# A two-layer decoder trunk: order of sums and passes in the second MLP matrix, zero-padded differential scores

## The chip, the cores and the metric

The kernel runs on one core of a Trainium2 chip. It is written with a tile framework whose scheduler decides the order of the instructions on each engine. The metric is the device time of one execution in microseconds; the kernel before takes 2158.03 us (median of 3 runs, 2157.67 to 2158.33).

## The reference

The input x is 256 positions by 2048 channels, in float32. Two layers each do the following (S = 256, D = 2048, hidden width 8192):

```python
h = rms_norm(x, attn_norm_g[l])
proj = h @ w_in[l]                      # 2048 -> 3*768 + 3*768 + 2*512
moba_o = moba_attention(...)            # 6 heads x 128, causal here, since one block of 256 holds all positions
diff_o = diff_attention(...)            # 6 heads, q and k in two halves of 64:
                                        # softmax(q1 k1 / 8) - lambda * softmax(q2 k2 / 8), then norm
sgu_o = spatial_gating(...)             # 4 groups x 128 channels, causal mixing in chunks of 128 positions
x = x + concat(moba_o, diff_o, sgu_o) @ w_out[l]
h = rms_norm(x, mlp_norm_g[l])
x = x + square(relu(h @ w_mlp_in[l])) @ w_mlp_out[l]
```

A last RMSNorm follows. All results are float32.

## The kernel before

**Products.** Every float32 operand of a large product is split into a high part, rounded to the matrix engine's own 32-bit form, and a low part, the rest. A product is then three matmul passes of 512 columns: high by high, low by high, high by low. `halves` (L115) makes the two parts of a piece of weights: ACT copies the high part (L122, tiles `hi_...`), DVE subtracts it from the raw weights (L123, tiles `lo_...`), for two k-tiles of 128 rows at a time (128x1024). The tiles come from pools of four buffers each (`whl`), so ACT and DVE can prepare only a few pieces ahead of the matmuls.

**The MLP in chunks.** The hidden width is worked off in four chunks c of 2048 per layer. A chunk takes two blocks (g = 0, 1) of the first matrix (tiles named `..._h`) and then two blocks of the second (tiles named `..._o`), each of 1024 columns, by `gemm7` (L173). Over two layers this makes 16 blocks of each matrix.

**The block.** A block has two row halves t (128 positions each) and two column halves of 512, so four accumulators, each a PSUM bank: `pz` (t 0, first columns), `py` (t 0, second columns), `px` (t 1, first) and `pw` (t 1, second). Eight of the sixteen k-tiles are taken in four pairs by a scheme with seven products in place of eight. Its weights b11, b12, b21, b22 are four raw tiles of 128x2048 in three buffers (`rb_...`), and four sums of them are made on DVE in place (L200): t1 = b11+b12, t2 = t1+b22, t3 = b12+b22, t4 = t2+b21. In the first matrix t3 is made by a DMA that accumulates (`moved=True`). The products go to px and py in turn; `keep` takes an intermediate result out of its bank before the bank is used again (`ks1`, `kv2`, `ks5` and `kv3`; on ACT for the first three, L699, and for v3 on DVE into ks5, L695). The other eight k-tiles are "plain" products: `plain(half, i)` takes two of them against one column half, and writes the two banks of that half, three passes for each bank and k-tile (L215 to L217). I write plain(1, 0) as k-tiles (1,0), and lo_o(1,0) is the low part that goes with it. The first pass of px in plain(0, 0) overwrites px, so it must wait until v3 has been taken from it.

The order of writing in `gemm7` is: product b11 into px; t1 into py; plain (1,0), (1,1); t2 into px; plain (1,2); b22 into py; plain (1,3); t3 into px; plain (0,0), (0,1); t4 into px; plain (0,2); b21 into pz; plain (0,3). After the block, the caller adds each bank to its result: in the second matrix to the residual stream `xt`, times a per-row factor (L705), then adds the kept parts to it (by a DMA of POOL's queue that accumulates, or on DVE in the last chunk, L711).

**Work between the passes.** `pending` holds generators; `pump()` advances one of them, between products. In an o g0 block the last hidden tiles of the first matrix are transposed on PE (L257), copied to their high parts on ACT (L96) and subtracted on DVE (L97): tiles `hid011a`, `hid011b` in layer 0, chunk 1.

**What sets the order.** Each instruction is given a priority by the place in which it is written, and the scheduler, with its own estimate of when operands come ready, puts on each engine the ready one that was written first. `tc.issue_after(x)` keeps what is written under it from being put into the queue before instruction x. Each engine then runs its queue strictly in order.

**Scores.** For each head, `turned_qk` (L472) transposes q and k on PE and copies both with one ACT instruction (L480). `scores` (L465) takes q times k in two passes (L468, L469). For the differential heads it does so twice, with 64 of the 128 rows (partitions) each.

Of the kernel before, what the change touches and what calls it, by code (L numbers as in the profile page):

```python
# [41 lines left out]
def trunk(ctx: ExitStack, tc: tile.TileContext, x_in, xT, w_in, w_out, w_mlp_in, w_mlp_out,  # L42
# [130 lines left out]
    def gemm7(w, c0, lhs, sums, rest, keep, name, moved=False):  # L173
# [31 lines left out]
        def plain(half, i):  # L205
# [4 lines left out]
            for k, (hi, lo) in zip(ks, halves(raw[half][:, i % 2 * 2:i % 2 * 2 + 2, :], 2, f"{name}{half}{i}")):  # L210
                a, h = lhs[k]
                for t, ps in enumerate(((pz, px), (py, pw))[half]):
                    ah, al = a[:, h, t * P:(t + 1) * P], a[:, h, S + t * P:S + (t + 1) * P]
                    first, last = k == rest[0] and t == half, k == ks[-1]
                    T.matmul(ps, lhsT=ah, rhs=hi, start=first, stop=False, skip_group_check=True)  # L215
                    T.matmul(ps, lhsT=al, rhs=hi, start=False, stop=False, skip_group_check=True)  # L216
                    T.matmul(ps, lhsT=ah, rhs=lo, start=False, stop=last, skip_group_check=True)  # L217
                pump()

        b11, b12 = rawb(0, 0), rawb(0, 1)  # L220
# [11 lines left out]
        product(px, summed(0), halves(b11, SP, f"t2{name}"))  # L232
        keep("v2", px)
        plain(1, 2)
        product(py, summed(1), halves(b22, SP, f"b22{name}"))
        if not moved:
            add(b12, b22)
        plain(1, 3)
# [7 lines left out]
        plain(0, 2)  # L246
        product(pz, direct(1, 0), halves(b21, SP, f"b21{name}"))
        plain(0, 3)
        return [[pz, py], [px, pw]]
# [90 lines left out]
    for l in range(DEPTH):  # L340
# [27 lines left out]
        tabs = att.tile([P, 2, 4, 64], F32, tag="tabs", name=f"tabs_{l}", bufs=1)  # L368
# [80 lines left out]
        vh, qt, kt = {}, {}, {}  # L449

# [21 lines left out]
        def turned_qk(sec, h, name):  # L472
# [319 lines left out]
```

## Time and profile before

| | us |
|---|---|
| median of 3 runs | 2158.03 |
| lowest, highest | 2157.67, 2158.33 |
| the profiled execution | 2156.94 |
| its span in the trace | 2155.2 |
| PE busy (9500 matmuls) | 2115.4 (98%) |
| DVE busy (2036 instructions) | 1717.3 (80%) |
| ACT busy (1891 instructions) | 1354.7 (63%) |
| POOL busy (78 instructions) | 65.3 (3%) |
| mean granted clock of PE | 0.997 |

PE is TensorE, DVE VectorE, ACT ScalarE and POOL GpSimd. A row of a timeline has the start from the span's begin, the duration, the engine, the line of the code, the result and its operands with their shape, and in brackets the idle time of the engine ahead of it with the instruction that ended it. Matmuls overlap: a pass of 512 columns is listed with 0.39 us, but the next one starts 0.23 us later, so it is differences of starts that count.

### The profile page before, as it was taken

Reading aid. Unit: us, or ns where it says so; the run is one execution under the profiler, and the core shown is the slowest. Engines: PE = TensorE matmul, PEld = TensorE weight load, DVE = VectorE, ACT = ScalarE, POOL = GpSimd, SP = SyncE. Lnnn points to the kernel's source line nnn. Section 1 sums busy time; section 2 is a strip of 40 time slices with the busy share of each in tenths; the row PEclk is TensorE's granted clock in tenths of the full one; section 3 lists DMA queues with packets and bytes.
Section 4 is the critical chain, followed back from the end, with each engine's and each line's share of the span. In section 5 each row is a group of like instructions: output and inputs, shape, how many; then the busy total and the mean of one; then the engine's idle time right before and its main releaser. Section 6 shows DMA issues by size and latency. Waiting matters only on the chain. (4 is left out here: it accounts for less than half of the span.)

```text
span 2155.2 us, 25746 instructions
## 1 busy us (share of the span) xinstructions
PE 2115.4 (98%) x9500; PEld 1707.6 (79%) x9500; DVE 1717.3 (80%) x2036; ACT 1354.7 (63%) x1891; POOL 65.3 (3%) x78
## 2 busy tenths in 40 slices
PE   9999999999999999999999999999999999999997
PEld 7877888877877887787788778888778778878875
DVE  6665566898898888889965655668988988988897
ACT  6565564675676576676654655556756756766764
POOL 0000000000000000000000000000000000000000
PEclk9999999999999999999999999999999999999998
DMA  8644565657866866775465455656677568668652
GB/s 320 197 154 147 174 220 182 196 177 229 259 186 190 266 208 200 217 227 195 153 212 187 137 166 166 224 167 197 209 229 235 176 215 256 203 190 251 213 195 98
DMA packets 210893, 432.20 MB, mean 201 GB/s; under 512 B 7632, under 2 KB 8272, under 8 KB 208592
## 3 DMA queue, kind: packets, MB, share of 16 engines
q1 hardware_dynamic: 202416, 402.22, 56.5%
q0 software_dynamic: 7488, 26.22, 6.2%
q10 hardware_dynamic: 864, 2.14, 0.3%
q8 instruction: 74, 1.21, 0.2%
q14 instruction: 51, 0.42, 0.1%
HBM read 402.23 MB, written 2.10 MB: 188 GB/s over the span
## 5 line engine op out<-in xcount | busy, mean ns | idle before, releaser
L123 DVE TENSOR_TENSOR lo_wi<-raw_wi,hi_wi 128x1024 fp32r<-128x1024 f32 x160 | 195.0, 1222 | 161.9 <-ACT hi_wi L122 158.8
L122 ACT ACTIVATE hi_wi<-raw_wi 128x1024 fp32r<-128x1024 f32 x160 | 168.8, 1058 | 166.6 <-PE pg_wi L157 158.1
L156 PE MATMUL pg_wi<-hi_wi,xa 128*128 128x512 f32 x640 | 260.6, 407 | 0.0
L158 PE MATMUL pg_wi<-lo_wi,xa 128*128 128x512 f32 x640 | 251.7, 393 | 0.0
L157 PE MATMUL pg_wi<-hi_wi,xa 128*128 128x512 f32 x640 | 251.4, 393 | 0.0
L122 ACT ACTIVATE hi_o<-raw_o 128x1024 fp32r<-128x1024 f32 x128 | 135.6, 1059 | 62.9 <-PE pw_o L216 36.7
L122 ACT ACTIVATE hi_h<-raw_h 128x1024 fp32r<-128x1024 f32 x128 | 135.3, 1057 | 43.1 <-PE px_h L216 20.6
L123 DVE TENSOR_TENSOR lo_o<-raw_o,hi_o 128x1024 fp32r<-128x1024 f32 x128 | 155.4, 1219 | 6.6 <-ACT hi_o L122 5.3
L123 DVE TENSOR_TENSOR lo_h<-raw_h,hi_h 128x1024 fp32r<-128x1024 f32 x128 | 155.0, 1216 | 3.7 <-ACT hi_h L122 3.7
L200 DVE TENSOR_TENSOR rb_o<-rb_o,rb_o 128x2048 f32<-128x2048 f32 x64 | 146.4, 2287 | 10.5 <-DMA rb_o<-w_mlp_out 10.0
L156 PEld LDWEIGHTS pg_wi<-hi_wi,xa 128*128 128x128 f32 x640 | 120.4, 188 | 29.0 <-issue 7.3
L158 PEld LDWEIGHTS pg_wi<-lo_wi,xa 128*128 128x128 f32 x640 | 120.4, 188 | 25.0
L157 PEld LDWEIGHTS pg_wi<-hi_wi,xa 128*128 128x128 f32 x640 | 120.6, 188 | 22.4 <-issue 0.7
L123 DVE TENSOR_TENSOR lo_wo<-raw_wo,hi_wo 128x1024 fp32r<-128x1024 f32 x64 | 78.4, 1225 | 60.8 <-ACT hi_wo L122 60.8
L200 DVE TENSOR_TENSOR rb_h<-rb_h,rb_h 128x2048 f32<-128x2048 f32 x48 | 109.7, 2286 | 0.6
L122 ACT ACTIVATE hi_wo<-raw_wo 128x1024 fp32r<-128x1024 f32 x64 | 67.9, 1060 | 64.0 <-PE pg_wo L157 58.0
L156 PE MATMUL pg_wo<-hi_wo,mix 128*128 128x512 f32 x192 | 76.3, 398 | 0.0
L158 PE MATMUL pg_wo<-lo_wo,mix 128*128 128x512 f32 x192 | 75.1, 391 | 0.0
L157 PE MATMUL pg_wo<-hi_wo,mix 128*128 128x512 f32 x192 | 74.8, 390 | 0.0
L123 DVE TENSOR_TENSOR lo_b11h<-rb_h,hi_b11h 128x1024 fp32r<-128x1024 f32 x32 | 39.2, 1225 | 27.8 <-ACT hi_b11h L122 25.8
L122 ACT ACTIVATE hi_b11h<-rb_h 128x1024 fp32r<-128x1024 f32 x32 | 34.0, 1063 | 33.9 <-PE px_h L216 13.3
L123 DVE TENSOR_TENSOR lo_t1h<-rb_h,hi_t1h 128x1024 fp32r<-128x1024 f32 x32 | 38.6, 1221 | 19.6 <-ACT hi_t1h L122 19.6
(1937 smaller groups left out, 5855.3 us busy)
## 6 DMA issues: line engine op xcount, KB each, us to landing
raw_wi<-w_in SPq DMA_DIRECT2D x80, 1024.0 KB, 5.2
rb_h<-w_mlp_in SPq DMA_DIRECT2D x64, 1024.0 KB, 5.8
raw_h<-w_mlp_in SPq DMA_DIRECT2D x64, 1024.0 KB, 7.0
raw_o<-w_mlp_out SPq DMA_DIRECT2D x64, 1024.0 KB, 6.6
rb_o<-w_mlp_out SPq DMA_DIRECT2D x64, 1024.0 KB, 6.4
raw_wo<-w_out SPq DMA_DIRECT2D x24, 1024.0 KB, 5.2
rb_h<-rb_h POOLq DMA_DIRECT2D x16, 1024.0 KB, 6.9
raw_wo<-w_out SPq DMA_DIRECT2D x16, 512.0 KB, 5.0
```

What stands on the lines that cost most here:

```text
L122: A.activation(hi, raw[:, i:i + m, :], AF.Copy)
L123: V.tensor_tensor(lo, raw[:, i:i + m, :], hi.bitcast(F32), op=ALU.subtract)
L156: T.matmul(ps[t], lhsT=ah, rhs=hi, start=first, stop=False)
L157: T.matmul(ps[t], lhsT=al, rhs=hi, start=False, stop=False)
L158: T.matmul(ps[t], lhsT=ah, rhs=lo, start=False, stop=last)
L200: V.tensor_tensor(dst, dst, src, op=ALU.add)
```

## The change

Four things change.

1. In `gemm7` of the second matrix (`moved` not set), the sum t3 = b12+b22 is no longer written after the product b22 but after `halves` of t2, under `issue_after`, so that it is queued behind the last low part of t2. `halves` notes that instruction in `last_lo`.
2. `plain` writes its passes in pieces of one k-tile and one bank. For i = 0 it takes both k-tiles for the bank that is free, and only then both for the other (`order`); for i > 0 k-tile by k-tile as before.
3. `gemm7` calls `second(py, pw)` when the second 512 columns are complete, after plain(0, 0) is written; the caller's `update(1, ...)` then adds py and pw to xt there, ahead of the sum t4 and not after the block. For the first matrix `second` only hands the banks back.
4. For the differential heads q goes into two tiles of 128 rows each, of which the other half's 64 rows are zero (`halfq`, set by four memsets per layer on POOL), by two ACT copies of 64x256, and k into a tile of its own, by one ACT copy of 128x256. `scores` then takes all 128 rows.

Besides, the scaled rotary table is written over the unscaled one.

```diff
@@ halves
-            V.tensor_tensor(lo, raw[:, i:i + m, :], hi.bitcast(F32), op=ALU.subtract)
+            made = V.tensor_tensor(lo, raw[:, i:i + m, :], hi.bitcast(F32), op=ALU.subtract)
...
+        last_lo[0] = made.ins
@@ gemm7, plain
-            for k, (hi, lo) in zip(ks, halves(...)):
-                a, h = lhs[k]
-                for t, ps in enumerate(((pz, px), (py, pw))[half]):
-                    (three passes)
-                pump()
+            parts = list(zip(ks, halves(...)))
+
+            def piece(k, hi, lo, t):
+                a, h = lhs[k]
+                ps = ((pz, px), (py, pw))[half][t]
+                (three passes)
+
+            order = [(0, 0), (0, 1), (1, 0), (1, 1)] if i else [(j, t) for t in (half, 1 - half) for j in (0, 1)]
+            for n, (j, t) in enumerate(order):
+                k, (hi, lo) = parts[j]
+                piece(k, hi, lo, t)
+                if n % 2:
+                    pump()
@@ gemm7, body
         plain(1, 0)
         plain(1, 1)
-        product(px, summed(0), halves(b11, SP, f"t2{name}"))
+        t2 = halves(b11, SP, f"t2{name}")
+        if not moved:
+            with tc.issue_after(last_lo[0]):
+                add(b12, b22)
+        product(px, summed(0), t2)
         keep("v2", px)
...
         product(py, summed(1), halves(b22, SP, f"b22{name}"))
-        if not moved:
-            add(b12, b22)
...
         plain(0, 0)
+        second(py, pw)
         add(b11, b21)
@@ differential scores
+        halfq = []
+        for i in range(2):
+            z = att.tile([P, 2, S], F32, tag=f"halfq{i}", name=f"halfq{l}{i}", bufs=1)
+            G.memset(z[64:, 0], 0.0)
+            G.memset(z[:64, 1], 0.0)
+            halfq.append(z)
...
+            if sec == "d":
+                z = halfq[h % len(halfq)]
+                k = stage["att"].tile([P, S], F32, tag="dk", name=f"dk_{name}", bufs=2)
+                for i, rows in enumerate((slice(0, 64), slice(64, P))):
+                    A.activation(z[rows, i], pT[rows, :S], AF.Copy)
+                A.activation(k, pT[:, S:], AF.Copy)
+                return z[:, 0], z[:, 1], k
@@ second matrix, caller
-                ps = gemm7(w2[...], ..., f"o{l}{c}{g}")
-                for half in (1, 0):
+                def update(half, ps, c=c, g=g, kept=kept, xg=xg):
...
+                update(0, gemm7(w2[...], ..., lambda *ps, update=update: update(1, ps), f"o{l}{c}{g}"))
```

What this does to the queues, in an o g0 block (layer 0, chunk 1). On DVE, from the last sum that the first matrix leaves to the low part of the second plain pair, the order before is this (`rb_o_5212` is b11 and the sums made in it, `rb_o_5214` is b12, `rb_o_5248` is b22):

```order
L678 TENSOR_TENSOR ks1h_4862<-ks1h_4862,pz_h_4826 128x512
L200 TENSOR_TENSOR rb_o_5214<-rb_o_5214,rb_o_5248 128x2048
L123 TENSOR_TENSOR lo_t1o_0_5251<-rb_o_5212,hi_t1o_0_5250 128x1024
L123 TENSOR_TENSOR lo_t1o_2_5255<-rb_o_5212,hi_t1o_2_5254 128x1024
L97 TENSOR_TENSOR hid011b_5269<-pT_hid011b_5264,hid011b_5269 128x2x256
L97 TENSOR_TENSOR hid011a_5283<-pT_hid011a_5278,hid011a_5283 128x2x256
L200 TENSOR_TENSOR rb_o_5212<-rb_o_5212,rb_o_5248 128x2048
L123 TENSOR_TENSOR lo_o_0_5292<-raw_o_5289,hi_o_0_5291 128x1024
L97 TENSOR_TENSOR hid011b_5306<-pT_hid011b_5301,hid011b_5306 128x2x256
L97 TENSOR_TENSOR hid011a_5320<-pT_hid011a_5315,hid011a_5320 128x2x256
L123 TENSOR_TENSOR lo_o_0_5324<-raw_o_5289,hi_o_0_5323 128x1024
```

And this is the order of the change there (b11 is `rb_o_5229`, b12 `rb_o_5231`, b22 `rb_o_5265`):

```order
L125 TENSOR_TENSOR lo_t1o_0_5268<-rb_o_5229,hi_t1o_0_5267 128x1024
L125 TENSOR_TENSOR lo_t1o_2_5272<-rb_o_5229,hi_t1o_2_5271 128x1024
L204 TENSOR_TENSOR rb_o_5229<-rb_o_5229,rb_o_5265 128x2048
L97 TENSOR_TENSOR hid011b_5286<-pT_hid011b_5281,hid011b_5286 128x2x256
L97 TENSOR_TENSOR hid011a_5300<-pT_hid011a_5295,hid011a_5300 128x2x256
L125 TENSOR_TENSOR lo_o_0_5309<-raw_o_5306,hi_o_0_5308 128x1024
L97 TENSOR_TENSOR hid011b_5323<-pT_hid011b_5318,hid011b_5323 128x2x256
L97 TENSOR_TENSOR hid011a_5337<-pT_hid011a_5332,hid011a_5337 128x2x256
L125 TENSOR_TENSOR lo_o_0_5341<-raw_o_5306,hi_o_0_5340 128x1024
L125 TENSOR_TENSOR lo_t2o_0_5357<-rb_o_5229,hi_t2o_0_5356 128x1024
L125 TENSOR_TENSOR lo_t2o_2_5361<-rb_o_5229,hi_t2o_2_5360 128x1024
L204 TENSOR_TENSOR rb_o_5231<-rb_o_5231,rb_o_5265 128x2048
```

The sum of b12 and b22 has gone from the place ahead of lo_t1 to the one behind the last lo_t2, and the sum for t2 has gone ahead of the two hid conversions.

On DVE further on in the same block, about the sum for t4 (with b21, `rb_o_5436`), the order before:

```order
L123 TENSOR_TENSOR lo_t3o_0_5417<-rb_o_5214,hi_t3o_0_5416 128x1024
L123 TENSOR_TENSOR lo_t3o_2_5421<-rb_o_5214,hi_t3o_2_5420 128x1024
L200 TENSOR_TENSOR rb_o_5212<-rb_o_5212,rb_o_5436 128x2048
L123 TENSOR_TENSOR lo_o_0_5444<-raw_o_5441,hi_o_0_5443 128x1024
L123 TENSOR_TENSOR lo_o_0_5461<-raw_o_5441,hi_o_0_5460 128x1024
L123 TENSOR_TENSOR lo_t4o_0_5477<-rb_o_5212,hi_t4o_0_5476 128x1024
L695 TENSOR_TENSOR ks5o_5287<-ks5o_5287,px_o_5208 128x512
L123 TENSOR_TENSOR lo_t4o_2_5481<-rb_o_5212,hi_t4o_2_5480 128x1024
```

And that of the change (b21 is `rb_o_5453`):

```order
L125 TENSOR_TENSOR lo_t3o_0_5434<-rb_o_5231,hi_t3o_0_5433 128x1024
L125 TENSOR_TENSOR lo_t3o_2_5438<-rb_o_5231,hi_t3o_2_5437 128x1024
L125 TENSOR_TENSOR lo_o_0_5461<-raw_o_5458,hi_o_0_5460 128x1024
L738 SCALAR_TENSOR_TENSOR xt_79<-py_o_5226,r_0_3494,xt_79 128x512
L738 SCALAR_TENSOR_TENSOR xt_80<-pw_o_5228,r_0_3494,xt_80 128x512
L204 TENSOR_TENSOR rb_o_5229<-rb_o_5229,rb_o_5453 128x2048
L729 TENSOR_TENSOR ks5o_5304<-ks5o_5304,px_o_5225 128x512
L125 TENSOR_TENSOR lo_o_0_5482<-raw_o_5458,hi_o_0_5481 128x1024
```

The updates of xt from py and pw now stand ahead of that sum, and ks5, which frees px, directly behind it.

On PE at the first plain passes of the same block, before:

```order
L169 MATMUL py_o_5209<-lo_t1o_2_5255,hid010b_4943 128x512
L215 MATMUL pw_o_5211<-hi_o_0_5291,hid011b_5269 128x512
L216 MATMUL pw_o_5211<-hi_o_0_5291,hid011b_5269 128x512
L215 MATMUL py_o_5209<-hi_o_0_5291,hid011b_5269 128x512
L216 MATMUL py_o_5209<-hi_o_0_5291,hid011b_5269 128x512
L167 MATMUL px_o_5208<-hi_t2o_0_5339,e_hid010a_4919 128x512
L217 MATMUL py_o_5209<-lo_o_0_5292,hid011b_5269 128x512
L217 MATMUL pw_o_5211<-lo_o_0_5292,hid011b_5269 128x512
```

And in the change the end of plain(1, 1) and the start of t2:

```order
L223 MATMUL py_o_5226<-lo_o_0_5341,hid011b_5323 128x512
L221 MATMUL pw_o_5228<-hi_o_0_5340,hid011b_5323 128x512
L222 MATMUL pw_o_5228<-hi_o_0_5340,hid011b_5323 128x512
L223 MATMUL pw_o_5228<-lo_o_0_5341,hid011b_5323 128x512
L170 MATMUL px_o_5225<-hi_t2o_0_5356,e_hid010a_4936 128x512
L171 MATMUL px_o_5225<-hi_t2o_0_5356,e_hid010a_4936 128x512
L172 MATMUL px_o_5225<-lo_t2o_0_5357,e_hid010a_4936 128x512
L170 MATMUL px_o_5225<-hi_t2o_0_5356,e_hid010a_4994 128x512
```

The first pass of t2 stood behind the first two passes of py; it now stands behind all passes of plain(1, 0) and plain(1, 1).

## Rows read from the trace of the kernel before

**Rows 1.** page part 1: busy us, share of the span, instructions.

```profile
PE 2115.4 (98%) x9500; PEld 1707.6 (79%) x9500; DVE 1717.3 (80%) x2036; ACT 1354.7 (63%) x1891; POOL 65.3 (3%) x78
```

**Rows 2.** windows: stretch, length, busy us (x count) per engine, PEclk, DMA.

```profile
593.50:637.40 43.90, 43.77 (x198) 35.18 (x198) 41.47 (x54) 33.65 (x45) 0.86 (x1) 1.00 0.67 200
637.40:683.50 46.10, 43.95 (x197) 35.24 (x196) 40.13 (x35) 29.43 (x34) 1.75 (x2) 1.00 0.64 205
```

**Rows 3.** waits of PE: line, releaser, total us, times, longest.

```profile
PE px_o L167 <- ACT hi_t2o L122: 10.1, 9, 1.3
PE px_o L215 <- DVE ks5o L695: 5.9, 15, 0.6
PE py_o L215 <- ACT ks5o L699: 3.0, 9, 1.2
```

**Rows 4.** timeline of PE, o g0: start us, duration, instruction, idle before.

```profile
645.30 0.39 PE L216 MATMUL pw_o<-hi_o,hid011b 128*128 128x512 f32 x1
645.93 0.50 PE L215 MATMUL py_o<-hi_o,hid011b 128*128 128x512 f32 x1 [0.23 <-ACT ks5o L699]
646.26 0.40 PE L216 MATMUL py_o<-hi_o,hid011b 128*128 128x512 f32 x1
647.88 0.50 PE L167 MATMUL px_o<-hi_t2o,e_hid010a 128*128 128x512 f32 x1 [1.22 <-ACT hi_t2o L122]
...
668.01 0.39 PE L216 MATMUL pz_o<-hi_o,hid011b 128*128 128x512 f32 x1
668.86 0.50 PE L215 MATMUL px_o<-hi_o,hid011b 128*128 128x512 f32 x1 [0.46 <-DVE ks5o L695]
```

**Rows 5.** timeline of ACT, the same block.

```profile
638.75 1.04 ACT L122 ACTIVATE hi_t1o<-rb_o 128x1024 fp32r<-128x1024 f32 x1
...
646.77 2.01 ACT L122 ACTIVATE hi_t2o<-rb_o 128x1024 fp32r<-128x1024 f32 x2
```

**Rows 6.** timeline of DVE, the same block.

```profile
638.79 2.28 DVE L200 TENSOR_TENSOR rb_o<-rb_o,rb_o 128x2048 f32<-128x2048 f32 x1
640.99 2.35 DVE L123 TENSOR_TENSOR lo_t1o<-rb_o,hi_t1o 128x1024 fp32r<-128x1024 f32 x2
...
644.46 2.28 DVE L200 TENSOR_TENSOR rb_o<-rb_o,rb_o 128x2048 f32<-128x2048 f32 x1
646.66 1.21 DVE L123 TENSOR_TENSOR lo_o<-raw_o,hi_o 128x1024 fp32r<-128x1024 f32 x1
...
652.40 1.21 DVE L123 TENSOR_TENSOR lo_o<-raw_o,hi_o 128x1024 fp32r<-128x1024 f32 x1
...
662.51 2.29 DVE L200 TENSOR_TENSOR rb_o<-rb_o,rb_o 128x2048 f32<-128x2048 f32 x1 [0.73 <-DMA rb_o<-w_mlp_out]
...
668.12 0.68 DVE L695 TENSOR_TENSOR ks5o<-ks5o,px_o 128x512 f32<-128x512 f32 x1
```

**Rows 7.** timeline of PE, o g1 of the same chunk.

```profile
709.76 0.39 PE L215 MATMUL pz_o<-hi_o,hid011b 128*128 128x512 f32 x1
710.38 0.50 PE L215 MATMUL px_o<-hi_o,hid011b 128*128 128x512 f32 x1 [0.23 <-DVE ks5o L695]
```

**Rows 8.** timeline of PE, last o g1 of layer 0.

```profile
1038.72 0.50 PE L215 MATMUL py_o<-hi_o,hid031b 128*128 128x512 f32 x1 [1.16 <-ACT ks5o L699]
```

**Rows 9.** timeline of PE around a score pair of 64 rows.

```profile
129.21 0.40 PE L158 MATMUL pg_wi<-lo_wi,xa 128*128 128x512 f32 x1
...
130.72 0.39 PE L157 MATMUL pg_wi<-hi_wi,xa 128*128 128x512 f32 x1
```

**Rows 10.** timeline of PE around a score pair of 128 rows.

```profile
237.12 0.40 PE L158 MATMUL pg_wi<-lo_wi,xa 128*128 128x512 f32 x1
...
238.23 0.39 PE L157 MATMUL pg_wi<-hi_wi,xa 128*128 128x512 f32 x1
```

**Rows 11.** groups of ACT by form: busy us, mean ns, idle before.

```profile
L480 ACT ACTIVATE qk_d<-pqk_d 128x512 f32<-128x512 f32 x12 | 6.9, 590 | 6.4 <-PE pqk_d L478 6.4
...
L96 ACT ACTIVATE mix<-po_m 128x256 fp32r<-128x256 f32 x12 | 4.5, 376 | 3.7 <-PE po_m L541 3.7
```

More of the change, by code (lines that the diff above doesn't have):

```diff
@@ L113, in load @@
         return raw
+    last_lo = [None]
     def halves(raw, n, name):
@@ L171, in product, with gemm7 @@
                 pump()
-    def gemm7(w, c0, lhs, sums, rest, keep, name, moved=False):
+    def gemm7(w, c0, lhs, sums, rest, keep, second, name, moved=False):
         def rawb(two, half):
@@ L209, in plain @@
             ks = rest[2 * i:2 * i + 2]
-            for k, (hi, lo) in zip(ks, halves(raw[half][:, i % 2 * 2:i % 2 * 2 + 2, :], 2, f"{name}{half}{i}")):
+            parts = list(zip(ks, halves(raw[half][:, i % 2 * 2:i % 2 * 2 + 2, :], 2, f"{name}{half}{i}")))
+            def piece(k, hi, lo, t):
                 a, h = lhs[k]
-                for t, ps in enumerate(((pz, px), (py, pw))[half]):
[L213 to L217, printed above, removed]
-                pump()
+                ps = ((pz, px), (py, pw))[half][t]
+                ah, al = a[:, h, t * P:(t + 1) * P], a[:, h, S + t * P:S + (t + 1) * P]
+                first, last = k == rest[0] and t == half, k == ks[-1]
+                T.matmul(ps, lhsT=ah, rhs=hi, start=first, stop=False, skip_group_check=True)
+                T.matmul(ps, lhsT=al, rhs=hi, start=False, stop=False, skip_group_check=True)
+                T.matmul(ps, lhsT=ah, rhs=lo, start=False, stop=last, skip_group_check=True)
+            order = [(0, 0), (0, 1), (1, 0), (1, 1)] if i else [(j, t) for t in (half, 1 - half) for j in (0, 1)]
[4 more added lines that the diff above has]
+                    pump()
+        n = len(rest) // 2
         b11, b12 = rawb(0, 0), rawb(0, 1)
@@ L231, in gemm7 @@
         plain(1, 1)
-        product(px, summed(0), halves(b11, SP, f"t2{name}"))
+        t2 = halves(b11, SP, f"t2{name}")
[3 more added lines that the diff above has]
+        product(px, summed(0), t2)
         keep("v2", px)
-        plain(1, 2)
+        for i in range(2, n - 1):
+            plain(1, i)
         product(py, summed(1), halves(b22, SP, f"b22{name}"))
-        if not moved:
-            add(b12, b22)
-        plain(1, 3)
+        plain(1, n - 1)
         product(px, summed(2), halves(b12, SP, f"t3{name}"))
@@ L245, in gemm7 @@
         product(px, direct(1, 1), halves(b11, SP, f"t4{name}"))
-        plain(0, 2)
+        for i in range(2, n - 1):
+            plain(0, i)
         product(pz, direct(1, 0), halves(b21, SP, f"b21{name}"))
-        plain(0, 3)
-        return [[pz, py], [px, pw]]
+        plain(0, n - 1)
+        return pz, px
     def turned(src, c, name, tag="m"):
@@ L265, in turn @@
             d = pair(f"{name}{i}")
-            if sums is not None and (k0 + i) // 2 < SP:
+            if sums is not None and (k0 + i) // 2 < len(sums):
                 a = stage["mlp"].tile([P, 2, S], F32, tag="a", name=f"a_{name}{i}", bufs=1)
@@ L365, in trunk @@
         rc = rstd(ss_a, f"a{l}")
-        tabs = att.tile([P, 2, 4, 64], F32, tag="tabs", name=f"tabs_{l}", bufs=1)
+        tabs = ropet
         for t in range(2):
@@ L463, in softmax, with scores @@
             return e, sm
-        def scores(qk, rows, name):
+        def scores(q, k, name):
             pS = bank(f"ps_{name}", "s")
-            q, k = qk[rows, :S], qk[rows, S:]
             T.matmul(pS[:, 0:P], lhsT=q[:, 0:P], rhs=k[:, 0:P], start=True, stop=True)
@@ L716, in trunk @@
                         pending.append(turn(xa, xt, q * GW, 4 * q, f"xa{l + 1}_{q}_", C_ATT + (l + 1) * KT))
+                update(0, gemm7(w2[c * fw:(c + 1) * fw], 2 * g * GW, Want(hid), Want(hs), late, keep,
+                                lambda *ps, update=update: update(1, ps), f"o{l}{c}{g}"))
         close_mlp.close()
```

29 lines of the change are left out of this document (15 added, 14 removed).

## Prediction

> **What bounds the kernel now.** I read the first part of the page first: TensorE (PE) is busy 2115.4 us of the span of 2155.2 [rows 1]. So there are 39.8 us in which no matmul runs, and a change can win only there, or where passes follow each other at more than their usual pitch. The second view is busy time by stretch, over one block of each of the two MLP matrices in layer 0, chunk 1: the second block of the first matrix, then the first block of the second matrix (I call the two blocks of the second matrix "o g0" and "o g1"). The two hold about the same matmuls, 198 and 197, and the granted clock is 1.00 in both; the first takes 43.90 us with PE busy 43.77, the second 46.10 with PE busy 43.95 [rows 2]. The reader is to see that an o g0 block has some 2.2 us of waits that its neighbour has not. DVE is busy 40.13 of those 46.10 us: it is not the bound on the mean, but every wait named next ends on an instruction that stands late in its queue or ACT's.
>
> The list of PE's waits says which [rows 3]: t2's first pass for ACT's hi_t2 (9 times, 10.1 us); px's first plain pass for DVE's ks5o, which reads that bank (15 times, 5.9); py's first plain pass for ACT's ks5o (9 times, 3.0). Eight o g0 blocks and one block at the layer's end make the nines, eight o g0 and seven o g1 the fifteen. The list gives idle time alone; what a wait costs I take from starts in the timeline, where 512-column passes otherwise follow at 0.23 us (43.77 us over 198 is 0.22, with some shorter transposes among them). In o g0: 645.30 to 645.93 is 0.63, so py costs 0.40; 646.26 to 647.88 is 1.62, so t2 costs 1.39; 668.01 to 668.86 is 0.85, so px costs 0.62 [rows 4]. The pass behind a wait starts 0.33 later instead of 0.23 (645.93, 646.26 in the same rows), so each wait costs 0.10 more.
>
> **Why those waits are there.** DVE starts the sum b12+=b22, which only t3 reads, at 638.79 and holds lo_t1 back to 640.99, though the first hi_t1 is finished at 638.75 + 1.04 = 639.79 [rows 5, 6]. The sum b11+=b22, from which t2 is made, starts at 644.46, and hi_t2 can only begin when it is done, at 646.77. Further on ks5o stands in DVE's queue behind the sum for t4, two lo_o and one lo_t4, and starts at 668.12. That sum waited 0.73 us for the load of b21 to land, and took 2.29 from 662.51.
>
> **Part 1: the sum for t3 behind t2's parts, and the pieces by bank (o g0).** Nothing is removed: the same add (2.2 us from start to next start) goes some ten places back. By the new order lo_t1 begins at 639.8, which is 1.2 earlier. The two lo_t1 take 2.3, and the two hid conversions behind them 1.2 (640.99 to 644.46 is 3.5 in all) [rows 6]. The new order puts the sum ahead of those conversions, so b11+=b22 begins at about 642.1 to 642.5 instead of 644.46, and ends 2 us earlier, before 644.7. hi_t2 is no longer what t2 waits for: t2's first pass now stands behind all 24 plain passes of k-tiles (1,0) and (1,1). The first of these with a lo part does wait, for lo_o(1,0). DVE reaches it behind two hid conversions, the second of which waits for an ACT copy that now stands behind two hi_o. I get 645.9 for lo_o's start against 646.66, and its end at about 647.2. PE asks for it after py's wait, which stays (ACT's ks5o keeps its time about: two hid copies have changed places with one hi_o, which nearly cancels). That is three passes past 645.93, about 646.4: a new wait of about 0.8. The bounds are no wait at all, and 1.39 as now; 0.8 lies nearest to what the queue gives. Gain: 1.39 - 0.8 = 0.6 per block.
>
> What is late next: lo_o(1,2), which now has the queued add in front of it. DVE goes on from 647.1 with two hid (1.2), one lo_o (1.15), lo_t2 twice (2.3), the add (2.2) and lo_o(1,2) (1.15): done at about 655.1. Before, it was started at 652.40. PE wants it at about 655.2 to 655.6. So there is hardly any margin, and I cost it at nothing; if that cover goes, each 0.1 us costs 0.8 us over the eight blocks. In o g1 there are no hid conversions on DVE, so there the margin is wide.
>
> **Part 2: the second 512 columns taken up early.** The two xt updates now stand ahead of the sum for t4, in time in which DVE waited for b21 anyway (0.73). ks5o comes straight after the sum: its end is 662.51 + 2.2 = 664.7 at the earliest. t3's last pass is through at about 666 in the new time, so ks5o (0.68) no longer waits for lo_o and lo_t4 in front, and is done some 0.3 us before px is needed, although px is asked for two passes (0.45) sooner, after six pz passes instead of eight. The px wait and its slower second pass go: 0.62 + 0.10 = 0.7 per block. Bounds: all 0.7, or the same 0.7 lost again if b21's load lands later. I take the gain.
>
> So 0.6 + 0.7 = 1.3 for the six o g0 blocks of chunks 0 to 2. In chunk 3 further sums into xt run on DVE (512 columns as ks5o's 0.68, one of them ahead of ks5o), so I take 0.95 for those two. 6 x 1.3 + 2 x 0.95 = 9.7 us.
>
> **Part 3: the same in o g1.** Its wait is px alone: 709.76 to 710.38 is 0.62, so 0.39, plus 0.10 [rows 7]. 0.5 x 6 = 3.0 for chunks 0 to 2. The last o g1 of layer 0 stands where the next layer's transposes begin: there py waited 1.16 by its row [rows 8]; of that and the shorter waits behind it I take 1.8 off. The last block of layer 1 I leave as it is. Sum 4.8. The first matrix's blocks keep their order but for a few pw pieces: 0, with 2 us either way.
>
> **Part 4: zero-padded scores.** A pair of score passes stands between two 512-column passes. With 64 rows (differential heads) the last pass ahead starts at 129.21 and the second behind at 130.72: 1.51 us [rows 9]. With 128 rows (the other heads), same columns, it is 237.12 to 238.23: 1.11 [rows 10]. The padded form has 128 rows, so 0.40 goes, 24 times (6 heads, 2 halves, 2 layers): 9.6 us. What it adds: ACT makes three copies per head instead of one of 590 ns. The nearest row, a 128x256 copy of 376 ns, gives at most 3 x 376 - 590 = 540 ns per head [rows 11]; ACT is busy 63%, and the score passes wait for these copies in few places. Bounds: 0, and 12 x 0.54 = 6.5 us if all of it were waited for; I take 0.8. Four memsets per layer on POOL run beside gemm passes: 0. The saved table changes no time. Part 4: 8.8 us.
>
> The Trainium skill speaks against this part. In "TensorE: Matmul & The Clock Gate", section "Why this matters for your kernels", it says that a single matmul with 32 rows of contraction takes the time of one with 128, and that only concurrent row groups gain. By that rule padding would give nothing, and the sum would be 14.5. The rows here show 0.40 between the two forms all the same; what differs is the start-to-start time around the pair, so the rule does not cover it. "TensorEngine Tiling (Array Packing)", section "Tiling Modes", has a rule for the other side: changing the tiling mode drains the engine. That fits the 0.40, though no row names a drain.
>
> **Sum.** 9.7 + 4.8 + 8.8 = 23.3 us off the profiled execution's own 2156.94 (span 2155.2 and 1.7 around it): 2133.6. That execution lies 1.1 below the median of the timed runs, 2158.03, so about 2134.
>
> **Rivals.**
> - *All waits of o g0 go.* If lo_o(1,0) is in time as well and py's wait shrinks, an o g0 block comes down to its neighbour's 43.90 and gains 2.2: 17.6 for eight, and the scores the full 9.6. 17.6 + 4.8 + 9.6 = 32: 2126; with the neighbour's own small waits gone also, 2120. For it: the same number of matmuls. Against it: ks5o on ACT keeps its place. Chance 0.17.
> - *The waits only move.* DVE is 0.7 us later than I reckon, the queued add delays lo_o(1,2) and takes back what t2 gave, and ks5o waits behind a sum that waits for b21. The MLP gains nothing, the scores 8.8: 2149. For it: DVE busy 87% of the block and a margin near zero. Chance 0.20.
> - *Padding gains nothing* (the 0.40 belongs to the place of these heads, not to their 64 rows). 23.3 - 8.8 = 14.5: 2143. Against it: no releaser is named in the 64-row rows. Chance 0.10.
> - *The queued add stands wholly in PE's way (slower).* If lo_o(1,2) waits for the add in all 16 blocks of the second matrix, at 2.2 each, this costs 35 us against the 23 gained: 2158 + 12 = 2170. It decides once DVE is more than 1.5 us behind PE's demand there, in o g1 too: from 16 x 1.5 = 24 on, the kernel is slower. Against it: o g1 has 2.4 us less DVE work before that place. Chance 0.03.
>
> My forecast has 0.50. Its own range is 2128 to 2140; with the rivals at 2126 to 2120, 2143 and 2149 the 8 in 10 lie in 2121 to 2149. About 0.2% (4.3 us) is what a measurement of this kernel can tell from no change. Every case but the slower one is 9 us or more faster; I leave 0.04 for no change, if the waits move and the copies are waited for too, and 0.04 for slower.
>
> **What would show it.** Right: the t2 wait on hi_t2 and the px wait on ks5o leave the list; a new wait on lo_o of about 0.8 us, eight times, stands in py's or pw's lo pass; o g0 blocks measure about 44.8 us; a differential score pair takes about 1.11 between its neighbours. Wrong: a wait of PE on lo_o in the third plain k-tile (the queued add), px still waiting for ks5o with the add waiting for b21's load, a score pair still at 1.5, or score passes waiting for the copies of dk.

## The result and the profile after

The changed kernel takes 2134.18 us (median of 4 runs, 2133.24 to 2134.84) against 2157.85 for the kernel before in the same session (2157.26 to 2158.33). The ratio is 0.989, 95% interval 0.9873 to 0.9907: faster by 23.7 us, where 23.3 were forecast and 2134 predicted.

The first part of the page, as in [rows 1]; matmuls are as many, and the time without any has shrunk from 39.8 to 26.7 us. That is 13.1 of the 22.1 us by which the span is shorter; the other 9.0 came off PE's own busy time (2115.4 to 2106.4), which no list of waits shows:

```profile
span 2133.1 us, 25737 instructions
PE 2106.4 (99%) x9500; PEld 1713.1 (80%) x9500; DVE 1718.1 (81%) x2036; ACT 1355.4 (64%) x1915; POOL 67.2 (3%) x86
```

The list of PE's waits, against [rows 3] (line, releaser, total us, times, longest):

```profile
PE pw_o L223 <- DVE lo_o L125: 5.1, 8, 0.6
...
PE px_o L221 <- DVE ks5o L729: 0.8, 1, 0.8
```

The three rows of before that made 19.0 us are down to one px wait, in the very last block. (Left out are two waits of 1.7 and 1.5 us at the kernel's start and five of 0.4 to 0.2; shorter ones do not stand in such a list, so that a wait of PE which falls into short pieces is not seen there.) In their place stands the one new wait that was forecast, for lo_o, eight times. Busy time by stretch (stretch, length, busy us and count of PE, PEld, DVE, ACT, POOL, granted clock, DMA share, GB/s), for the o g0 block that answers to [rows 2] and the o g1 block behind it, and first that o g1 block in the kernel before:

```profile
683.50:725.20 41.70, 41.47 (x181) 33.51 (x180) 37.92 (x32) 25.05 (x26) 2.58 (x3) 1.00 0.72 224
```

```profile
632.80:677.60 44.80, 44.03 (x198) 35.34 (x197) 40.31 (x35) 29.04 (x34) 1.72 (x2) 1.00 0.65 207
677.60:718.80 41.20, 41.20 (x181) 33.60 (x180) 37.85 (x32) 24.94 (x26) 2.58 (x3) 1.00 0.72 230
```

46.10 has become 44.80, and 41.70 has become 41.20. Inside the o g0 block PE's timeline, against [rows 4]:

```profile
640.89 0.50 PE L222 MATMUL pw_o<-hi_o,hid011b 128*128 128x512 f32 x1
641.35 0.50 PE L221 MATMUL py_o<-hi_o,hid011b 128*128 128x512 f32 x1
641.69 0.40 PE L222 MATMUL py_o<-hi_o,hid011b 128*128 128x512 f32 x1
642.72 0.50 PE L223 MATMUL pw_o<-lo_o,hid011b 128*128 128x512 f32 x1 [0.63 <-DVE lo_o L125]
...
651.11 0.39 PE L223 MATMUL py_o<-lo_o,hid011a 128*128 128x512 f32 x1
...
662.39 0.39 PE L223 MATMUL pz_o<-lo_o,hid011b 128*128 128x512 f32 x1
662.61 0.39 PE L221 MATMUL px_o<-hi_o,hid011b 128*128 128x512 f32 x1
```

641.69 to 642.72 is 1.03, so the new wait is 0.80 beyond the usual 0.23. py comes 0.46 after the pass before it, where it was 0.63. px follows its forerunner at 0.22: it does not wait at all. DVE in the same block, against [rows 6]:

```profile
641.45 1.22 DVE L125 TENSOR_TENSOR lo_o<-raw_o,hi_o 128x1024 fp32r<-128x1024 f32 x1
...
647.18 2.28 DVE L204 TENSOR_TENSOR rb_o<-rb_o,rb_o 128x2048 f32<-128x2048 f32 x1
649.39 1.22 DVE L125 TENSOR_TENSOR lo_o<-raw_o,hi_o 128x1024 fp32r<-128x1024 f32 x1
...
659.32 2.28 DVE L204 TENSOR_TENSOR rb_o<-rb_o,rb_o 128x2048 f32<-128x2048 f32 x1
661.52 0.68 DVE L729 TENSOR_TENSOR ks5o<-ks5o,px_o 128x512 f32<-128x512 f32 x1
```

A lo_o that starts at 641.45 releases PE at 642.72, which is 1.27 later. The queued sum starts at 647.18, lo_o(1,2) behind it at 649.39, so its pass could go at 650.66; PE comes to it at 651.11. That is 0.45 us to spare. The sum for t4 no longer shows a wait for b21's load, and ks5o stands directly behind it.

A score pair of a differential head, against [rows 9]:

```profile
129.34 0.40 PE L161 MATMUL pg_wi<-lo_wi,xa 128*128 128x512 f32 x1
...
130.45 0.39 PE L160 MATMUL pg_wi<-hi_wi,xa 128*128 128x512 f32 x1
```

129.34 to 130.45 is 1.11, as for the heads with 128 rows [rows 10]; it was 1.51. The copies on ACT that answer to [rows 11]:

```profile
L508 ACT ACTIVATE halfq<-pqk_d 64x256 f32<-64x256 f32 x24 | 9.0, 375 | 6.5 <-PE pqk_d L502 6.4
L509 ACT ACTIVATE dk_d<-pqk_d 128x256 f32<-128x256 f32 x12 | 4.6, 385 | 0.1
```

### The profile page after: what moved, and what is told of

It is laid out like the page before. It is cut to its first block, busy times and chain, and to the rows that moved or that the text cites. A ratio compares the mean times of both kernels' runs of the same rounds, so it can differ in the third digit from the quotient of the medians.

```text
span 2133.1 us, 25737 instructions
## 1 busy us (share of the span) xinstructions
PE 2106.4 (99%) x9500; PEld 1713.1 (80%) x9500; DVE 1718.1 (81%) x2036; ACT 1355.4 (64%) x1915; POOL 67.2 (3%) x86
## 4 chain that ended last, share of the span: by engine, by line
PE 83%; issue 8%; DVE 6%; ACT 2%; DMA 1%; POOL 0%; POOLq 0%; ACTq 0%; SPq 0%; DVEq 0%
PE pg_wi L161 7%; PE pg_wi L159 7%; PE pg_wi L160 7%; PE pg_wo L159 3%; PE pg_wo L161 3%; PE pg_wo L160 3%; PE px_h L172 2%; PE px_h L170 2%; PE px_h L171 2%; PE px_o L172 2%; PE px_o L171 2%; PE px_o L170 2%; PE px_h L221 1%; PE px_h L223 1%; PE px_h L222 1%
## 5 line engine op out<-in xcount | busy, mean ns | idle before, releaser
L124 ACT ACTIVATE hi_t4o<-rb_o 128x1024 fp32r<-128x1024 f32 x32 | 33.7, 1054 | 34.8 <-DVE rb_o L204 34.8
```

Source lines behind the costliest of these rows:

```text
L124: A.activation(hi, raw[:, i:i + m, :], AF.Copy)
```

## Experiments

In all of them "the whole change" is the changed kernel, 2134.2 us. The kernel before stood at 2157.9 to 2159.5 in the four sessions, so differences under some 2 us between sessions say little; where a few tenths matter I use block lengths, taken from start to start of the blocks' first passes in the profiles.

### Padding alone

The three parts of the MLP undone in the changed kernel, so that the zero-padded scores are left, with what belongs to them (the rotary table written in place, two buffers instead of four for `qk`):

```diff
-        if not moved:
-            with tc.issue_after(last_lo[0]):
-                add(b12, b22)
         product(px, summed(0), t2)
...
         product(py, summed(1), halves(b22, SP, f"b22{name}"))
+        if not moved:
+            add(b12, b22)
...
-            order = [(0, 0), (0, 1), (1, 0), (1, 1)] if i else [(j, t) for t in (half, 1 - half) for j in (0, 1)]
+            order = [(0, 0), (0, 1), (1, 0), (1, 1)]
...
-        second(py, pw)
         add(b11, b21)
...
         plain(0, n - 1)
+        second(py, pw)
```

> The zero-padded scores (with the scaled rotary table written in place) alone; the sum t3, the pieces and the updates are as in the kernel before. My theory: the passes of 24 differential pairs lose about 0.39 us each (9.4) and the three ACT copies give 1 to 2 back, so 2150 us, with the MLP blocks at their old lengths (o g0 46.1, o g1 41.8). Rival: the gain of the changed kernel is all in the MLP and the padding is worth nothing: 2157 to 2158. Second rival: padding gives more than its pairs, since other attention work moves up: below 2147.

Measured: 2150.33 against 2158.34, ratio 0.9964 (0.995 to 0.9978), 8.0 us. The waits of PE in the MLP are the old ones:

```profile
PE px_o L170 <- ACT hi_t2o L124: 10.0, 9, 1.3
PE px_o L221 <- DVE ks5o L728: 5.6, 15, 0.5
```

So padding is worth 8 us by itself, and "padding gains nothing" is refuted.

### Everything but the queued sum

```diff
-        if not moved:
-            with tc.issue_after(last_lo[0]):
-                add(b12, b22)
...
         product(py, summed(1), halves(b22, SP, f"b22{name}"))
+        if not moved:
+            add(b12, b22)
```

> The whole change without its first part: the sum t3 = b12+b22 is written after the product b22 as in the kernel before. My theory: this part carries nearly the whole MLP gain, the px wait's as well as the t2 wait's, because ks5o then stands behind two lo_o again: about 2149 to 2151, the same as with padding alone, with the waits for hi_t2 (about 10 us) and for ks5o (4 to 6 us) back in the list of PE's waits. Rival: the early update of xt frees px and the bank order adds to it, so only the t2 wait comes back: 2138 to 2142.

Measured: 2143.68, ratio 0.9934 (0.9919 to 0.9949). That is between the theory's number and the upper end of the rival's. My theory holds in o g0 and fails in o g1. The list of PE's waits shows the one for t2 back, and only four of the fifteen for px:

```profile
PE px_o L170 <- ACT hi_t2o L124: 9.7, 8, 1.2
...
PE px_o L221 <- DVE ks5o L728: 1.7, 4, 0.8
```

o g0 blocks are at 45.95 to 46.15 as before (the one at the end of layer 0 at 46.83), but o g1 blocks at 41.27 to 41.29 in five of six: their px wait is gone without the queued sum. In o g0 it is not gone, though the list has few of them. It stands there in two pieces, too short for the list:

```profile
664.70 0.39 PE L222 MATMUL pz_o<-hi_o,hid011b 128*128 128x512 f32 x1
665.12 0.50 PE L223 MATMUL pz_o<-lo_o,hid011b 128*128 128x512 f32 x1
665.71 0.50 PE L221 MATMUL px_o<-hi_o,hid011b 128*128 128x512 f32 x1
```

These passes come 0.42 and 0.59 after the ones before them, so 0.55 beyond the usual pitch, against 0.57 in one piece with padding alone. DVE's order is the reason: in the o g0 blocks of this run it still takes the sum for t4 first, with lo_o, the xt updates and (in six of the eight) another lo_o ahead of ks5o; in o g1 the sum stands behind lo_o and the updates, and ks5o directly behind the sum.

### The queued sum alone (with padding)

The changed kernel with the old pass order and `second` called after the block (the last two pieces of the first diff).

> Padding and the first part (the sum t3 queued behind t2's parts), with the updates of xt after the block and the old pass order. My theory: 2134 to 2138, within 4 us of the whole change; o g0 blocks 44.8 to 45.1 us, o g1 41.3 to 41.6. Rival: the early update is what frees px, so the px waits (0.7 in eight o g0 blocks, 0.5 in seven o g1) come back: 2142 to 2144.

Measured: 2144.41, ratio 0.9936 (0.9921 to 0.9951): the rival's figure, but for 0.4. The t2 wait is gone and the px waits are all there:

```profile
PE py_o L223 <- DVE lo_o L125: 5.1, 8, 0.6
PE px_o L221 <- DVE ks5o L729: 4.6, 15, 0.6
```

o g0 blocks take 45.3 to 45.5 (0.7 less than with padding alone), o g1 41.9 to 42.1 (nothing less).

### The early update alone (with padding)

The changed kernel with the sum t3 at its old place and the old pass order; only `second` stands behind plain(0, 0).

> Padding and the early update of xt alone; the sum t3 and the pass order are as in the kernel before. The runs so far: padding alone 2150.3, everything but the queued sum 2143.7. Theory: the early update by itself takes the px waits out of o g1 (0.65 in seven blocks) and 2 to 3 us out of the block at the end of layer 0, and in o g0 nothing, since there ks5o still stands behind two lo_o: 2143 to 2145. Rival: it is the bank order that does this, and the early update alone gives nothing: 2149 to 2151.

Measured: 2144.0, ratio 0.9935 (0.992 to 0.9949), as the theory had it. o g1 blocks take 41.27 to 41.32 in five of six, o g0 46.04 to 46.5 in layer 1. This kernel's one profile was taken in an execution of 2148.34 us, with two o g0 blocks of 47.7 and 47.8 in layer 0 in which the clock fell (see the end); the other three runs lie at 2143.91 to 2144.04.

### The whole change with the old pass order

```diff
-            order = [(0, 0), (0, 1), (1, 0), (1, 1)] if i else [(j, t) for t in (half, 1 - half) for j in (0, 1)]
+            order = [(0, 0), (0, 1), (1, 0), (1, 1)]
```

> The whole change with the old pass order in the first plain pair. Theory: px is asked for after five pz passes instead of six, 0.23 us sooner, and the changed kernel has 0.36 us to spare there (ks5o starts at 661.52, a pass that waits for it starts 0.73 later, px stands at 662.61): so nothing is lost, 2133 to 2136. Rival: the bank order carries the px gain together with the early update, and without it 0.5 us come back in each of 15 blocks: 2140 to 2143.

Measured: 2134.85, ratio 0.9888 (0.9873 to 0.9902). Nothing that can be told from the whole change; o g0 blocks take 44.81 to 44.87 (45.81 at the end of layer 0, as in the whole change). The bank order is worth nothing that these runs can tell.

### 64-row pairs next to each other, in the kernel before

```diff
-            e0, s0 = softmax(scores(qk, slice(0, 64), n + "a"), 0.125, n + "a")
+            p0 = scores(qk, slice(0, 64), n + "a")
+            p1 = scores(qk, slice(64, 128), n + "b")
+            e0, s0 = softmax(p0, 0.125, n + "a")
             yield
-            e1, s1 = softmax(scores(qk, slice(64, 128), n + "b"), 0.125, n + "b")
+            e1, s1 = softmax(p1, 0.125, n + "b")
```

> The kernel before, with 64 rows as there, but both score pairs of a differential head issued next to each other, the softmaxes behind them. It tells apart what the 0.39 us are paid for. If a pass of 64 rows costs more by itself, or each pair does, nothing is gained: 2157 to 2158, and a stretch of four score passes takes about 1.11 + 0.88 + 2 x 0.39. If it is paid where passes of 64 rows follow on passes of 128 rows and the other way (entering and leaving), it is paid once per head and 12 x 0.39 = 4.7 us go: about 2153, and the stretch of four takes 0.39 less than that.

Measured: 2151.92 against 2158.34, ratio 0.9971 (0.9961 to 0.9981), 6.4 us, more than the 4.7 expected. PE's timeline shows why, at a head whose two pairs stand together:

```profile
150.45 0.40 PE L158 MATMUL pg_wi<-lo_wi,xa 128*128 128x512 f32 x1
150.77 0.37 PE L468 MATMUL ps_d04a<-qk_d 64*128 64x128 f32 x1
150.79 0.37 PE L468 MATMUL ps_d04b<-qk_d 64*128 64x128 f32 x1
...
151.98 0.40 PE L157 MATMUL pg_wi<-hi_wi,xa 128*128 128x512 f32 x1
```

The passes of the two halves start 0.01 to 0.02 us apart, two by two, and all of them together take 150.45 to 151.98, 1.53 us, as a single pair of 64 rows did (1.51 [rows 9]). The second pair is free. That is what the Trainium skill says in "TensorE: Matmul & The Clock Gate", section "Why this matters for your kernels": passes on separate row groups run at the same time, and the gain lies in that. The trace agrees that they run at the same time. That nothing else gains is not borne out: a lone 64-row pair among 128-row passes takes 0.40 us more than a padded one (1.51 and 1.11), and the padding alone gave 8.0 us. Only half of the heads (three of six in layer 0) came to stand so; the scheduler put other passes between the rest.

### The sum t2 queued later

The whole change, and in the second matrix t2's sum behind the low part of plain(1, 0), to take the 0.80 us wait away:

```diff
-        add(b11, b22)
+        if moved:
+            add(b11, b22)
         keep("s5", py)
...
         plain(1, 0)
+        if not moved:
+            with tc.issue_after(last_lo[0]):
+                add(b11, b22)
         plain(1, 1)
```

> The whole change, and in the second matrix also the sum t2 = t1+b22 queued behind the low part of the first plain pair. Theory: DVE then makes lo_o(1,0) some 2 us earlier, the wait of 0.80 us for it goes in eight o g0 blocks, and about 0.3 of it comes back at lo_o(1,2), which has two sums in front of it: 2129 to 2132. Rival: DVE, busy nearly without a gap there, only passes the wait on in full, to lo_o(1,2) or ks5o: 2133 to 2136.

Measured: 2137.67, ratio 0.9901 (0.9886 to 0.9916), 3.5 above the whole change. lo_o(1,0) now starts at 638.81 and PE has it in time; but the wait is back in full, and more, at lo_o(1,2), which has both sums in front of it (rows of DVE with the two sums, then the row of PE):

```profile
637.86 0.69 DVE L97 TENSOR_TENSOR hid011b<-pT_hid011b,hid011b 128x512 fp32r<-128x512 f32 x1 [0.56 <-ACT hid011b L96]
638.81 1.23 DVE L125 TENSOR_TENSOR lo_o<-raw_o,hi_o 128x1024 fp32r<-128x1024 f32 x1 [0.26 <-ACT hi_o L124]
639.95 2.28 DVE L204 TENSOR_TENSOR rb_o<-rb_o,rb_o 128x2048 f32<-128x2048 f32 x1
...
647.35 2.28 DVE L204 TENSOR_TENSOR rb_o<-rb_o,rb_o 128x2048 f32<-128x2048 f32 x1
649.55 1.21 DVE L125 TENSOR_TENSOR lo_o<-raw_o,hi_o 128x1024 fp32r<-128x1024 f32 x1
```

```profile
650.82 0.50 PE L223 MATMUL py_o<-lo_o,hid011a 128*128 128x512 f32 x1 [0.86 <-DVE lo_o L125]
```

DVE reaches lo_o(1,2) no sooner (649.55 against 649.39), though this block starts 0.6 us earlier in the profile (632.16 against 632.77). Up to there it has the same work, and 0.8 us more of waiting: where the sum for t2 stood, DVE now waits 0.56 and 0.26 us for copies of ACT, and the sum comes later, ahead of parts that PE asks for next. o g0 blocks take 45.3 instead of 44.8.

### Both sums queued later

As the last, with `add(b12, b22)` under `issue_after` of plain(1, 2)'s low part.

> As the last, with the sum t3 queued behind lo_o(1,2) instead of t2's parts. Theory: lo_o(1,2) is then in time too and the whole 0.80 us goes in eight blocks: 2127 to 2129. Rival: the wait moves to lo_b22, t3 or ks5o, since DVE's work up to there is the same: 2131 to 2136.

Measured: 2132.99, ratio 0.9878 (0.9861 to 0.9894), 1.2 below the whole change and not to be told from it. The rival holds: the wait has moved on to px.

```profile
661.87 0.39 PE L222 MATMUL pz_o<-hi_o,hid011b 128*128 128x512 f32 x1
662.62 0.50 PE L221 MATMUL px_o<-hi_o,hid011b 128*128 128x512 f32 x1 [0.37 <-DVE ks5o L733]
```

```profile
651.00 2.35 DVE L125 TENSOR_TENSOR lo_b22o<-rb_o,hi_b22o 128x1024 fp32r<-128x1024 f32 x2
...
659.68 2.29 DVE L204 TENSOR_TENSOR rb_o<-rb_o,rb_o 128x2048 f32<-128x2048 f32 x1 [0.47 <-DMA rb_o<-w_mlp_out]
661.89 0.68 DVE L733 TENSOR_TENSOR ks5o<-ks5o,px_o 128x512 f32<-128x512 f32 x1
```

PE comes 0.5 us too early there, because DVE's sum for t4 (659.68, after 0.47 us of waiting for b21's load) is no earlier than in the whole change (659.32), though the waits ahead are gone. That load hangs on DVE itself: b21 is the fourth tile in three buffers, and its load is issued at 653.38, when DVE has finished lo_b22o (651.00 and 2.35 us), which stands behind both sums. In eight of the profiles, read at this place, the issue follows lo_b22o's end within 0.1 us, and the load lands 6.2 to 6.3 us later. o g0 blocks stay at 44.7 to 44.9 (45.57 at the end of layer 0).

### The sum t3 by a DMA

The whole change, but b12+b22 of the second matrix is made by POOL's accumulating DMA as in the first:

```diff
-        if moved:
-            G.dma_start(b12, b22, accum_op=ALU.add)
+        G.dma_start(b12, b22, accum_op=ALU.add)
...
-        if not moved:
-            with tc.issue_after(last_lo[0]):
-                add(b12, b22)
```

> The whole change, but the sum t3 of the second matrix is made by an accumulating DMA of POOL's queue, as in the first matrix: 16 sums of 2.2 us leave DVE. Theory: in the changed kernel that sum is hidden (0.45 us to spare at lo_o(1,2), 0.36 at ks5o), and the wait of 0.80 us that is left stands in front of it in DVE's queue, so nothing moves: 2132.5 to 2135. Rival: the sum, though queued late, still delays something in each block, and its going gives 0.5 us or more in 16 blocks: below 2127. Second rival: the 16 added transfers delay the loads: above 2136.

Measured: 2145.55, ratio 0.9939 (0.9924 to 0.9954), 11.4 above the whole change. That is the figure of the second rival (above 2136), but its mechanism does not show: b21's load, which DVE waits for, lands 24.6 us into the o g0 block of chunk 1, and in the whole change at 26.4. PE has a new wait in pz's pass with lo_o (five times, 1.7 us), and DVE's timeline in o g0 shows the reason:

```profile
658.64 2.29 DVE L204 TENSOR_TENSOR rb_o<-rb_o,rb_o 128x2048 f32<-128x2048 f32 x1 [0.75 <-DMA rb_o<-w_mlp_out]
660.85 1.22 DVE L125 TENSOR_TENSOR lo_o<-raw_o,hi_o 128x1024 fp32r<-128x1024 f32 x1
661.99 0.75 DVE L734 SCALAR_TENSOR_TENSOR xt<-py_o,r,xt 128x512 f32<-128x512 f32 x1
...
664.44 0.68 DVE L725 TENSOR_TENSOR ks5o<-ks5o,px_o 128x512 f32<-128x512 f32 x1
```

The scheduler has put the sum for t4 first again, ahead of lo_o and the xt updates; it waits 0.75 us for b21's load, and lo_o, the updates, another lo_o and ks5o stand behind it. o g0 blocks take 45.4 to 45.6, o g1 42.0 to 42.4. So where t3's sum stands also decides the order about t4's. In all o g0 blocks of the runs in which t3's sum is queued on DVE, lo_o and an xt update come before the sum for t4; without it (at its old place, or by DMA) lo_o or the updates come after it. In o g1 t3's sum has this effect from its old place too, and only the DMA turns the order round. What the scheduler goes by is not shown; my reading is that it counts DVE as free when t3's sum is gone.

### The sum t2 queued later and t3 by a DMA

The last two edits together.

> The sum t2 queued behind the low part of the first plain pair, and the sum t3 off DVE by a DMA. It tells whether DVE's amount of work sets the length of an o g0 block, which stayed at 44.8 us with t2 late, the wait being passed on to ks5o. Theory: with 2.2 us less on DVE nothing takes the wait's place, o g0 comes to 43.9 to 44.2 and the whole to 2126 to 2129. Rival: what passes the wait on is the order or the load of b21, not DVE's load: ks5o is still late, o g0 stays at 44.8, 2132 to 2135.

Measured: 2135.57, ratio 0.9893 (0.9879 to 0.9908). The total is 0.6 above the rival's range, and its reason is not what happened. An o g0 block and the o g1 behind it:

```profile
632.20:676.50 44.30, 44.15 (x198) 35.15 (x197) 38.17 (x34) 29.03 (x34) 2.59 (x3) 1.00 0.77 239
676.50:718.65 42.15, 41.74 (x181) 33.52 (x180) 35.99 (x31) 25.27 (x26) 3.47 (x4) 1.00 0.83 237
```

With 2.2 us less on DVE (38.17 against 40.31) o g0 comes to 44.2 to 44.3 in seven blocks, 0.5 below the whole change, and the lo_o wait is not passed on: there DVE's amount of work was what passed it on. But o g1, at 42.1 to 42.3, is 0.9 longer, by the same order as in the run before: its sum for t4 starts after 1.0 us of waiting for b21's load, with lo_o, both xt updates, a second lo_o and ks5o behind it. In five of the six o g1 blocks this costs 0.7 to 1.1, which uses up the 0.5 to 0.6 that each of the eight o g0 blocks gains.

### The changed MLP with 64-row pairs next to each other

The changed kernel with the padded scores taken out and the two pairs written together, as in the run above.

> The changed MLP with scores of 64 rows as in the kernel before, the two pairs of a head next to each other instead of zero-padded. In the run of that alone, where two pairs stood next to each other their passes started 0.01 us apart (150.77, 150.79) and the four took 1.53 us together, as one pair did; half of the heads stood so, and it gave 6.4 us against 8.0 of the padding. Theory: the parts add up, so 2134.2 + 8.0 - 6.4 = 2135.8, 2134 to 2137. Rival: the padding's gain comes with waits for its three copies that weigh more beside the other changes: at or below 2133.

Measured: 2136.35 (2135.54 to 2138.08), ratio 0.9896 (0.9879 to 0.9912), as the theory had it. The padding is at least as good as the scheduler's half-way pairing, and the parts add up.

### All three variants together

t2 late, t3 by DMA and 64-row pairs next to each other.

> t2 late, t3 by DMA and the scores of 64 rows with pairs next to each other, no padding. Each part as before: by the sum of the parts 1.6 us above the run with t2 late and t3 by DMA with padding. Theory: 2128 to 2130 if that one has 2126 to 2129. Rival: pairs next to each other ask for two banks at once and delay the transposes that want them, and lose more: above 2132.

Measured: 2138.78 (2136.7 to 2141.2), ratio 0.9909 (0.9894 to 0.9924). Its forecast hung on 2126 to 2129 for the run without the pairs; against the 2135.57 that this run gave, it is 3.2 more, with 1.6 expected and a spread of 4.5. The rival's figure (above 2132) was already passed without the pairs, so it says nothing for the rival. No version that was run is faster than the changed kernel by more than the measurement can tell.

## Why the prediction was right

**The t2 wait and what took its place.** Forecast: 1.39 goes, a new wait of about 0.8 for lo_o(1,0) comes, 0.6 per block. Measured: 0.80 beyond the pitch, eight times, and 0.7 per o g0 block with the queued sum alone. lo_o was put at 645.9, which is 0.76 ahead of its old start in a block that starts at 637.40, so 8.5 us into it; it started 641.45 - 632.80 = 8.65 us in. Py's wait, which was to stay, fell from 0.40 to 0.23.

**px.** Forecast: ks5o done 0.3 us before it is needed, 0.7 per o g0 block. Where px does wait, it starts 0.73 after ks5o's start (661.89 and 662.62 in the run with both sums later; 663.12 and 663.85 in the queued-sum run). In the changed kernel ks5o starts at 661.52, so px could go at 662.25 and goes at 662.61: 0.36 to spare. From the queued sum alone (45.3 to 45.5) to the whole change (44.8) is 0.5 to 0.7. The forecast gave this to the early update. The runs say so for o g1, where it takes the wait away by itself. In o g0 it takes both edits: the early update alone gives nothing (46.0 and more against 46.0 to 46.1), the queued sum alone takes nothing off px, and together they give all of it, because only then ks5o stands directly behind the sum for t4. My later theory, that the queued sum carries it, was wrong too.

The forecast's other bound, that the gain is lost if b21's load lands later, came near. The load is issued when lo_b22o is done, and the queued sum stands ahead of that:

```profile
652.90 0.37 SPq L188 DMA_DIRECT2D rb_o<-w_mlp_out  x1
```

This is 20.1 us into the block, which starts at 632.77; before, the load was issued 18.9 us in (656.26 and 637.38). It lands 6.3 us later, at 26.4, and the sum for t4 starts at 26.55. So b21 did come 1.3 us later, and the two xt updates fill that time.

**Per block.** 1.3 forecast, 46.10 to 44.80 measured. In the two blocks of chunk 3, 0.95 each was forecast: 0.42 (46.21 to 45.79) and 1.32 (46.16 to 44.84), 1.74 for 1.9. In o g1, 0.5 for each of six blocks: five gained 0.50 to 0.71, the first lost 0.23 (a wait for lo_t1 of 0.4), together 2.8 for 3.0. From the start of the last o g1 of layer 0 to the next layer's first pass 45.70 became 44.06, 1.6 where 1.8 was taken, of which the rows had shown 1.16.

**The queued sum's danger.** The margin at lo_o(1,2) was called hardly any; it is 0.45. The slower rival, the sum in PE's way in all 16 blocks, did not come about; its mechanism is real all the same, since the t2-late run, which put one more sum ahead of it, shows 0.86 us of idle time at just that pass.

**Scores.** Per pair 0.40 was forecast, and 1.51 has become 1.11. The term that was mis-sized is the price of the copies: 0.8 us was taken. The attention section, from the first pass of its second product to the first of the output projection, went from 256.45 to 252.66 us in layer 0 and from 256.44 to 252.65 in layer 1, 3.79 each. 24 pairs at 0.39 would be 9.4; 7.6 came, so 1.8 went elsewhere. Most of it is at the first pairs of two heads in each layer, which wait for dk_d, the third copy:

```profile
125.74 0.40 PE L160 MATMUL pg_wi<-hi_wi,xa 128*128 128x512 f32 x1
126.37 0.49 PE L492 MATMUL ps_d02a<-dk_d,halfq 128*128 128x128 f32 x2 [0.23 <-ACT dk_d L509]
```

The first score pass comes 0.63 after the pass ahead, where 0.23 is usual. With the slower starts behind it and the second of the two heads this is 0.7 us per layer by the starts, 1.3 in all; the other 0.5 was not traced. Score passes that wait for the copies were one of the prediction's signs of being wrong; they are there, in this size. The three copies take 2 x 375 + 385 = 1135 ns per head against 590, and the estimate of 376 for each was right.

**Sum.** MLP 14.5 and scores 8.8 were forecast. The trace has 14.1 from the MLP sections (from the first matrix's first pass to the next layer's first pass, 697.07 to 690.20, and in layer 1 to the last px pass, 694.45 to 687.26), 7.6 from attention, and 0.8 from the first product of layer 1: 22.4 in all, less 0.2 lost at the start; the spans differ by 22.1. That the total came within 0.4 us of the timed difference owes something to luck: the scores came 1.2 short, and 0.8 came from a place for which the forecast had no term.

## What to carry to other kernels

A sum in an in-order queue costs what stands behind it, not its own length: 2.2 us of work were moved ten places back at no price, because DVE reached the next thing that PE wanted 0.45 us early, and because other work filled the 1.3 us by which the next load came later. When a queue has hardly a gap, moving one piece only hands the wait to the next place, and the place is found by following the queue to each instruction that the other engine asks for, and to each buffer that it frees for a load. A list of waits can lose a wait that falls into short pieces; the length of the block does not. Where a scheduler sets the order, taking work away can also turn its order for the worse (11 us with t3's sum by DMA), so the new order has to be read before the gain is reckoned.

## What the runs showed of the hardware

- Passes of 64 rows on the two halves of the array, issued next to each other, start 0.01 to 0.02 us apart and the second pair costs nothing; a lone 64-row pair among 128-row passes costs 0.40 us over a 128-row one.
- The granted clock fell in the one profile of the early-update run, in two o g0 blocks of layer 0, right behind the place of the t2 wait:

```profile
640.00:645.00 5.00, 4.09 (x20) 2.81 (x18) 5.00 (x5) 4.99 (x9) 0.00 (x0) 1.00 0.01 3
645.00:648.00 3.00, 2.43 (x8) 1.95 (x9) 3.00 (x5) 1.46 (x2) 0.00 (x0) 0.77 0.00 0
648.00:650.50 2.50, 2.50 (x9) 1.92 (x8) 2.50 (x3) 1.06 (x1) 0.00 (x0) 0.59 0.51 149
```

PE was busy 4.09 of the 5 us from 640 to 645, and its first t2 pass came at 645.57, 1.64 after the pass before it. From 646.62 on passes of 512 columns followed at 0.43 instead of 0.23 us, the lower of the two levels (1.2 GHz), and from 650.01 on at 0.23 to 0.25 again, the upper one (2.4 GHz). The block took 47.77 us for 46.1. Other profiles have a wait of this size at the same place with the clock at 1.00 ([rows 2, 4]), so this hangs on more than the runs here tell apart.
